# Block 1's values made 512 columns wide in six PSUM banks, the first key tile ahead of them, the gating in the last step and behind

## The chip, the cores and the metric

The kernel runs on one core of a Trainium2 chip. TensorE (PE) multiplies into PSUM, VectorE (DVE), ScalarE (ACT) and GpSimd (POOL) do the elementwise work, and SyncE's queue (SP) issues nearly all of the transfers. The metric is the device time of one execution in microseconds, as the median of several runs.

## What is computed

Two transformer blocks on 512 positions of 1024 channels, in fp32. The change is in the first block. `h` is the normalised, modulated input and `hc` the same for a context of 256 positions. From `h` come queries, keys, values and the inputs of a spatial gating and of a convolution; from `hc` come keys and values only. Cut to what matters:

```
h  = _modulate(_rmsnorm(x, norm1_g[l]), mod_l[0], mod_l[1])
hc = _modulate(_rmsnorm(xc, norm1_g[l]), mod_c[0], mod_c[1])
z  = h @ w_in[l]
q, k, v = _heads(z[..., :ATT_W]), _heads(z[..., ATT_W:2*ATT_W]), _heads(z[..., 2*ATT_W:3*ATT_W])
kvc = hc @ w_in[l][:, ATT_W:3 * ATT_W]
kc, vc = _heads(kvc[..., :ATT_W]), _heads(kvc[..., ATT_W:])
att = _neighbourhood_attention(q, k, v, kc, vc, na_rpb[l], rows)
y   = _mix_out(att, z, ...)      # joins att, the gating and the convolution
```

Here `ATT_W` is 512 (8 heads of 64). The gating mixes positions within chunks of 128 by a learned matrix and multiplies the result by `gelu(u)`; the convolution has 31 taps for each channel.

## The kernel before

**Precision and weights.** Every fp32 product is made of three matmuls (`mm3`): each operand is split into a high half (ScalarE, a copy to fp32r) and a low half (VectorE, the difference), and high by high, high by low and low by high are summed in a PSUM bank. The weights come through a stream `ws`: pieces of up to 1 MB are loaded by SP into `wraw`, and units of 128 by 1024 numbers are split into `whi` and `wlo`. `need(u)` asks for units two ahead of the one in use and loads one or two pieces beyond, in the order in which the `Proj` objects were made.

**Order.** The program is written out by hand; each engine works through its instructions in that order. PSUM has eight banks, given out by `bank()` from one pool; a bank is reused when the last reader of its former tile is done. Work that has no place of its own, above all the 62 convolution taps (`tap_v`, on VectorE, tile `cacc`), lies in a list `lv`, and `tick(part)` puts some of it into the order: at the rate of this stage, 3.3 x part / 0.75 taps.

**The stage in question.** Two tiles of queries for each of two weight pieces are projected. Between them `make_hc(*ks)` builds `hc[k]`: VectorE scales the context `cs`, ScalarE writes the high half, VectorE the low one; the last call makes `hc[5]` to `hc[7]` behind the last query tile. `ada_tick` puts eight modulation matmuls (`adab`) between. Then come the values. They are made in two halves of 256 columns, in tiles of 128 positions: four from `h` and two from `hc` for each half, each tile 8 steps of `mm3` in a bank of its own and split at once (`v_tile`). `split(*vn[i], vt_[i])` prepares the gating's operand, `gating(0)` and `gating(1)` each put 12 matmuls into two `mix` banks, add a bias on VectorE (tile `sgo`) and multiply by `u` on GpSimd. The generator `keys()` makes four tiles of keys, each step three matmuls with `h[k]` (512 columns, bank `k`) and three with `hc[k]` (256 columns, bank `kc`). Its first tile is taken ahead of the fourth tile of the second half, the others are spread over the attention, three or two steps a turn. Between the value tiles stand twelve copies of half tiles on GpSimd (`vs`), which shift values by 64 positions.

**The attention** runs over 32 turns (8 heads, 4 blocks). Turn n does the scores (`s`), the softmax (VectorE, ScalarE; GpSimd scales tile `e` by the reciprocal sum), and three turns later TensorE transposes it (`pt`). Everything on GpSimd goes in the order written.

Of the kernel before, what the change touches and what calls it, by code (L numbers as in the profile page):

```python
# [15 lines left out]
P = 128  # L16
T = 512
D = 1024
KD = D // P
# [112 lines left out]
def program(ctx: ExitStack, tc: tile.TileContext, A, outT):  # L132
# [14 lines left out]
    def bank(name="bank", cols=T):  # L147
        return ps.tile([P, cols], F32, tag="b", name=name, padded_shape=[P, T])

    def slot(dt=F32, name="slot", cols=T):  # L150
        t = sl.tile([P, T], dt, tag="s", name=name)
        return t if cols == T else t[:, :cols]

    def pair(name, cols=T):
        return slot(F32R, name + "_hi", cols), slot(F32R, name + "_lo", cols)


    def mm3(out, lhs, rhs, start, stop, **kw):

        PE.matmul(out, lhs[0], rhs[0], start=start, stop=False, **kw)  # L160
        PE.matmul(out, lhs[0], rhs[1], start=False, stop=False, **kw)  # L161
        PE.matmul(out, lhs[1], rhs[0], start=False, stop=stop, **kw)  # L162

    def split(hi, lo, src, scale=None, eng=None):

        if scale is None:
            S.activation(hi, src, AF.Copy)  # L167
            (eng or V).tensor_sub(lo, src, hi)  # L168
        else:
            S.activation(hi, src, AF.Copy, scale=scale)  # L170
            V.scalar_tensor_tensor(lo, src, scale, hi, op0=ALU.mult, op1=ALU.subtract)
# [49 lines left out]
    ws = Stream()  # L221
# [58 lines left out]
    def take(gen, n):  # L280

        for _ in range(n):
            if next(gen, None) is None:
                return

    class Later:
# [8 lines left out]
        def tick(self, part=1.0):  # L295
            self.due += self.rate * part
            while self.todo and self.due >= self.todo[0][0]:
                cost, fn, a = self.todo.pop(0)
                self.due -= cost
                fn(*a)  # L300
            if not self.todo:
                self.due = 0.0
# [44 lines left out]
    def doubled(parts):  # L347

        out = [(a, slot(F32R, "dbl")) for a in parts]
        for a, b in out:  # L350
            move(b[TOP], a[LOW])
            move(b[LOW], a[LOW])
        yield 1
        for a, b in out:
            move(a[LOW], a[TOP])
        yield out

    def stacked(hi, lo, other):

        move(other[TOP], hi[LOW])  # L360
        move(other[LOW], lo[LOW])
        yield 1
        move(hi[LOW], lo[TOP])
        yield hi, other
# [3 lines left out]
    def put_later(to, i, gen):  # L368

        left = [1]  # L370
        to[i] = None

        def step():
            if left:
                left.pop()
                return
            r = next(gen)
            if r != 1:
                to[i] = r
                later.remove(step)  # L380

        later.append(step)
# [22 lines left out]
    w_in, w2 = A["w_in"], A["w_in_2"]  # L405
    p_u = Proj(w_in, 1536, 8)
    p_q = [Proj(w_in, 256 * i, 8) for i in range(2)]
    p_v = [Proj(w_in, 1024 + 256 * i, 8, wide=True) for i in range(2)]
    p_k = [Proj(w_in, 512 + 256 * i, 8) for i in range(2)]
    p_out = [Proj(A["w_out"], 256 * i, 8) for i in range(4)]  # L410
    p_up = [[Proj(A["ffn_w_up"], c + 256 * j, 8) for c in (0, FF)] for j in range(KF // 2)]
    p_down = [Proj(A["ffn_w_down"], 256 * i, KF) for i in range(4)]
# [40 lines left out]
    def pc(name, i, n=1):  # L453
        a = PCOL[name][0]
        return par[:, a + i : a + i + n]
# [49 lines left out]
    h = [None] * KD  # L505
# [84 lines left out]
    def ada_end():  # L590
        r, t = ada_ends.pop(0)
        b = ada_bank.pop(r)
        for q in range(4):
            PE.matmul(b[:, 4 * q : 4 * q + 4], t[:, q * P : (q + 1) * P], pick, start=True, stop=True)
        for g in (0, 2):
            j = 4 * ROUNDS[r][g]
            V.tensor_add(mod[:, j : j + 8].rearrange("p (g q) -> p g q", q=4),
                         b[:, :16].rearrange("p (q g) -> p g q", g=4)[:, g : g + 2],
                         pc("ada_b", j, 8).rearrange("p (g q) -> p g q", q=4))
# [3 lines left out]
    def ada_tick(n=2):  # L603

        if ada_ends:
            ada_end()
        for _ in range(min(n, len(ada_live))):
            ada_step()
            ada_fetch()
# [138 lines left out]
    vt_ = []  # L748
    for i in range(4):
        b = bank("vgT", cols=256)  # L750
# [9 lines left out]
    hc = [None] * KD  # L760
# [19 lines left out]
    vn = []  # L780
# [15 lines left out]
    def gating(pr):  # L796
        for n2 in range(2):
            b = bank("mix")
            for n in range(2):
                lhs = [vn[2 * n2 + n][q][:, pr * P : (pr + 1) * P] for q in range(2)]  # L800
                mm3(b[:, n * 256 : (n + 1) * 256], lhs, [q[:, pr * 256 : (pr + 1) * 256] for q in sgp], True, True)
            for gg in range(2):
                r = slice(64 * gg, 64 * gg + 64)
                bv = b.rearrange("p (n g q) -> p g n q", n=2, g=2)[r, gg]
                ov = sgo[pr].rearrange("p (n q) -> p n q", q=P)[r, 2 * n2 : 2 * n2 + 2]
                bb = rows[1][r, pr * P : (pr + 1) * P].unsqueeze(1).to_broadcast([64, 2, P])
                V.tensor_add(ov, bv, bb)
        G.tensor_mul(sgo[pr], sgo[pr], u[pr])
# [17 lines left out]
    vt = [pair(f"v{i}") for i in range(4)]  # L826
    vc = [pair(f"vc{i}") for i in range(2)]
    vs = [pair(f"vs{i}") for i in range(3)]

    def keys():  # L830
        for i in range(4):
            b, bc_ = bank("k"), bank("kc", cols=CTX)
            for k in range(KD):
                w_ = p_k[i // 2].part(i % 2, k)
                mm3(b, w_, h[k], k == 0, k == KD - 1)
                mm3(bc_, w_, hc[k], k == 0, k == KD - 1)
                yield 6
            nat, other = pair("k"), slot(F32R, "k")
            split(*nat, b)
            t = slot(F32R, "kc")  # L840
            kcp[i] = t[:, :CTX], t[:, CTX:]
            for o, r in zip(kcp[i], (TOP, LOW)):
                split(o[TOP], o[LOW], bc_[r])

            put_later(kp, i, stacked(*nat, other))
            if i == 0:
                put_later(qp, i, doubled(qp[i]))
            tick(1.5 if i else 0)
        h.clear()
        hc.clear()  # L850

    def v_tile(pj, half, src, i, dst):
        cols = slice(256 * half, 256 * half + 256)
        b = bank("v", cols=256)
        for k in range(KD):
            mm3(b, [src[k][q][:, i * P : (i + 1) * P] for q in range(2)], pj.part(0, k, 256), k == 0, k == KD - 1)
        split(dst[0][:, cols], dst[1][:, cols], b)
        tick(0.5)

    for i in range(4):  # L860
        v_tile(p_v[0], 0, h, i, vt[i])
        split(*vn[i], vt_[i])
        if i % 2:
            ada_tick()
    for i in range(2):
        v_tile(p_v[0], 0, hc, i, vc[i])
    kg = keys()

    ws.limit = p_k[0].at[0, 0][0] + 1
    for i in range(4):  # L870
        if i == 3:
            take(kg, KD + 1)
        v_tile(p_v[1], 1, h, i, vt[i])
        if i in (0, 2):
            gating(i // 2)
        if i == 1:
            ada_end()
    for i in range(3):
        for q in range(2):
            G.tensor_scalar(vs[i][q][0:64, :], vt[i][q][64:128, :], 1.0, 0.0, op0=ALU.mult, op1=ALU.add)  # L880
            G.tensor_scalar(vs[i][q][64:128, :], vt[i + 1][q][0:64, :], 1.0, 0.0, op0=ALU.mult, op1=ALU.add)
    for i in range(2):
        v_tile(p_v[1], 1, hc, i, vc[i])
    ws.limit = 1 << 30
    del vn, sgp, vg, vt_, xs
    cs.clear()

# [150 lines left out]
    for n in range(NA + OUT + 2):  # L1038
        if n < NA:
            hp, blk, j = place(n)  # L1040
            if n in QD:
                i = 1 + QD.index(n)
# [37 lines left out]
        for i, steps in PLAN.get(n, ()):  # L1080
            if len(begun) == i:
                b = bank()
# [336 lines left out]
    for n in range(32 + O2 + 2):  # L1419
# [17 lines left out]
        q = n - O2  # L1437
# [201 lines left out]
```

## Time and profile before

| | |
|---|---|
| median of 3 runs | 1387.32 us (1387.29 to 1387.36) |
| profiled execution | 1388.53 us, its span 1386.1 us |
| TensorE busy | 1371.3 us (99% of the span) |
| VectorE, ScalarE, GpSimd busy | 778.7, 560.1, 228.4 us |
| mean granted TensorE clock | 0.997 |

The span runs from the first to the last instruction that the profiler saw; the execution's own time is 2.4 us more. A busy share counts an engine as busy from the start of an instruction to its end, and matmuls overlap, so two matmuls that start 0.23 us apart may each be 0.39 us long. How fast TensorE goes is seen by the distance from start to start. The stage of the change lies between 100 and 180 us of the span.

### The profile page before, as it was taken

How to read it: one execution, taken by the hardware profiler on the slowest of the kernel's cores; microseconds unless marked ns; L12 is line 12 of the kernel's file. 1: busy time of each engine (PE TensorE's matmuls, PEld its weight loads, DVE VectorE, ACT ScalarE, POOL GpSimd, SP SyncE). 2: the span in 40 equal slices, each digit the busy share in tenths (PEclk: the TensorE clock that was granted, in tenths of full speed). 3: DMA queues.
4: the chain of work that ended last, by engine and by line, in shares of the span. 5: the costliest groups of instructions: out<-in, count | busy, mean ns of one | idle time of the engine just before them, and what ended most of it. 6: DMA issues, size and time to landing. Idle time of an engine off the chain costs nothing.

```text
span 1386.1 us, 18747 instructions
## 1 busy us (share of the span) xinstructions
PE 1371.3 (99%) x7468; PEld 1151.3 (83%) x7468; DVE 778.7 (56%) x1158; ACT 560.1 (40%) x901; POOL 228.4 (16%) x252
## 2 busy tenths in 40 slices
PE   9999999999999999999999999999999999999997
PEld 5768999898888888888888888888897888888887
DVE  4479788465444443434458863635378866663223
ACT  4433258445333333323355543323454544343231
POOL 0032324101111110111133312000231111110100
PEclk9999999999999999999999999999999999999998
DMA  9992452323232222322273122333212332222221
GB/s 347 367 370 95 116 140 67 122 92 98 85 122 92 91 93 83 106 85 91 84 199 109 51 92 76 107 111 102 92 62 68 123 113 93 91 84 84 84 84 61
DMA packets 140886, 160.41 MB, mean 116 GB/s; under 512 B 5632, under 2 KB 117504, under 8 KB 140800
## 3 DMA queue, kind: packets, MB, share of 16 engines
q1 hardware_dynamic: 139360, 156.91, 35.1%
q10 hardware_dynamic: 1440, 2.31, 0.5%
q8 instruction: 58, 0.95, 0.3%
q14 instruction: 28, 0.23, 0.1%
HBM read 147.67 MB, written 2.10 MB: 108 GB/s over the span
## 4 chain that ended last, share of the span: by engine, by line
PE 88%; issue 4%; DVE 4%; POOL 2%; ACT 1%; DMA 1%; POOLq 0%; ACTq 0%
PE bank L160 23%; PE bank L162 23%; PE bank L161 23%; PE first L565 3%; PE v L160 1%; PE v L162 1%; PE v L161 1%; PE adab L484 1%; PE s L907 1%; PE pt L935 1%; DMA ada<-in_ada_first 1%; DVE wlo L209 1%; PE f L160 1%; PE f L161 1%; PE f L162 1%
## 5 line engine op out<-in xcount | busy, mean ns | idle before, releaser
L209 DVE TENSOR_TENSOR wlo<-wraw,whi 128x1024 fp32r<-128x1024 f32 (+1 forms) x211 | 276.0, 1316 | 117.2 <-ACT whi L201 117.0
L162 PE MATMUL bank<-h_hi,wlo 128*128 128x512 f32 (+1 forms) x816 | 304.2, 373 | 1.7 <-DVE wlo L209 1.7
L161 PE MATMUL bank<-h_lo,whi 128*128 128x512 f32 (+1 forms) x816 | 305.6, 374 | 0.2
L160 PE MATMUL bank<-h_hi,whi 128*128 128x512 f32 (+1 forms) x816 | 305.0, 374 | 0.0
L201 ACT ACTIVATE whi<-wraw 128x1024 fp32r<-128x1024 f32 (+1 forms) x211 | 217.1, 1035 | 99.3 <-PE bank L161 85.2
L160 PEld LDWEIGHTS bank<-h_hi,whi 128*128 128x128 f32 x816 | 153.6, 188 | 30.1 <-PE adab L484 1.7
L162 PEld LDWEIGHTS bank<-h_hi,wlo 128*128 128x128 f32 x816 | 153.6, 188 | 29.5 <-DVE wlo L209 2.5
L161 PEld LDWEIGHTS bank<-h_lo,whi 128*128 128x128 f32 x816 | 153.5, 188 | 28.1 <-DVE h_lo L1505 0.3
L168 POOL TENSOR_TENSOR act_lo<-cv,act_hi 128x512 fp32r<-128x512 f32 x44 | 61.3, 1393 | 428.9 <-ACT act_hi L167 428.9
L160 PE MATMUL bank<-act_hi,whi 128*128 128x512 f32 x308 | 119.8, 389 | 0.0
L161 PE MATMUL bank<-act_lo,whi 128*128 128x512 f32 x308 | 119.8, 389 | 0.0
L162 PE MATMUL bank<-act_hi,wlo 128*128 128x512 f32 x308 | 119.8, 389 | 0.0
L160 PE MATMUL bank<-hb_hi,whi 128*128 128x512 f32 x288 | 115.9, 403 | 0.3 <-DVE wt_lo L1400 0.3
L162 PE MATMUL bank<-hb_hi,wlo 128*128 128x512 f32 x288 | 112.6, 391 | 0.0
L161 PE MATMUL bank<-hb_lo,whi 128*128 128x512 f32 x288 | 112.5, 391 | 0.0
L167 ACT ACTIVATE act_hi<-cv 128x512 fp32r<-128x512 f32 x44 | 27.8, 633 | 129.4 <-DVE cv L1230 73.0
L161 PEld LDWEIGHTS bank<-act_lo,whi 128*128 128x128 f32 x308 | 57.8, 188 | 12.1
L162 PEld LDWEIGHTS bank<-act_hi,wlo 128*128 128x128 f32 x308 | 57.8, 188 | 12.0
L160 PEld LDWEIGHTS bank<-act_hi,whi 128*128 128x128 f32 x308 | 57.8, 188 | 11.9
L162 PEld LDWEIGHTS bank<-hb_hi,wlo 128*128 128x128 f32 x288 | 54.1, 188 | 11.6
L160 PEld LDWEIGHTS bank<-hb_hi,whi 128*128 128x128 f32 x288 | 54.1, 188 | 10.1 <-DVE wt_lo L1400 0.4
L161 PEld LDWEIGHTS bank<-hb_lo,whi 128*128 128x128 f32 x288 | 54.2, 188 | 9.1
(388 smaller groups left out, 2412.9 us busy)
## 6 DMA issues: line engine op xcount, KB each, us to landing
wraw<-in_w_in SPq DMA_DIRECT2D x23, 1024.0 KB, 5.5
wraw<-in_ffn_w_up SPq DMA_DIRECT2D x22, 1024.0 KB, 5.1
wraw<-in_w_up SPq DMA_DIRECT2D x22, 1024.0 KB, 5.1
ada<-in_ada_w SPq DMA_DIRECT2D x64, 256.0 KB, 5.7
ada<-in_ada_first SPq DMA_DIRECT2D x32, 256.0 KB, 6.0
wraw<-in_w_out SPq DMA_DIRECT2D x8, 1024.0 KB, 5.0
wraw<-in_ffn_w_down SPq DMA_DIRECT2D x8, 1024.0 KB, 5.0
wraw<-in_w_down SPq DMA_DIRECT2D x8, 1024.0 KB, 5.3
```

What stands on the lines that cost most here:

```text
L160: PE.matmul(out, lhs[0], rhs[0], start=start, stop=False, **kw)
L161: PE.matmul(out, lhs[0], rhs[1], start=False, stop=False, **kw)
L162: PE.matmul(out, lhs[1], rhs[0], start=False, stop=stop, **kw)
L167: S.activation(hi, src, AF.Copy)
L168: (eng or V).tensor_sub(lo, src, hi)
L201: S.activation(h, src, AF.Copy)
L209: V.tensor_sub(l, src, h)
L484: PE.matmul(out[32 * g : 32 * g + 32, : rhs.shape[1]], sc[:, kk, :], rhs, start=start, stop=stop, tile_position=(0, 32 * g), skip_group_ch ...
L565: PE.matmul(first[m], w_[:, m * P : (m + 1) * P], h[k][a], start=s0 and k == 0, stop=s1 and k == KD - 1)
L907: PE.matmul(st_s[n][:, ks], qp[hp][a][j][:, qs], k_, start=a == 0, stop=a == 1)
L935: PE.transpose(pt[:, c * P : (c + 1) * P], e[:, c * P : (c + 1) * P], ident)
```

## The change

The values become one projection of 512 columns: for each of the 8 steps, six `mm3` into six banks, four from `h` and two from `hc`. All six tiles are split behind the last step. The key weights are cut into pieces of 128, 128 and 256 columns, with the first ahead of the values, and the whole first key tile (its splits too) stands ahead of the values; a `yield 0` keeps the second tile's first step out of it. The splits of `vn` go into the first four value steps, `ada_tick` behind the steps 1 and 3, `ada_end` behind 5, `gating(0)` behind step 6, and `gating(1)` behind the splits of the values. `tick(0.75)` eight times takes the place of `tick(0.5)` twelve times. The limit on the weight stream in this stage falls away.

```diff
-    p_v = [Proj(w_in, 1024 + 256 * i, 8, wide=True) for i in range(2)]
-    p_k = [Proj(w_in, 512 + 256 * i, 8) for i in range(2)]
+
+    p_k = [Proj(w_in, 512, 8, P)]
+    p_v = Proj(w_in, 1024, 8, 512, wide=True)
+    p_k += [Proj(w_in, 512 + P, 8, P), Proj(w_in, 768, 8)]
+    k_tile = (p_k[0], 0), (p_k[1], 0), (p_k[2], 0), (p_k[2], 1)
...
-                w_ = p_k[i // 2].part(i % 2, k)
+                w_ = k_tile[i][0].part(k_tile[i][1], k)
...
             tick(1.5 if i else 0)
+            if i == 0:
+                yield 0
...
-    for i in range(4):
-        v_tile(p_v[0], 0, h, i, vt[i])
-        split(*vn[i], vt_[i])
-        if i % 2:
+    kg = keys()
+    take(kg, KD + 1)
+    vb = [bank("v") for _ in range(6)]
+    for k in range(KD):
+        w_ = p_v.part(0, k, 512)
+        for i, b in enumerate(vb):
+            mm3(b, [q[:, i % 4 * P : (i % 4 + 1) * P] for q in (h if i < 4 else hc)[k]], w_, k == 0, k == KD - 1)
+        if k < 4:
+            split(*vn[k], vt_[k])
+        if k in (1, 3):
             ada_tick()
-    for i in range(2):
-        v_tile(p_v[0], 0, hc, i, vc[i])
-    kg = keys()
-
-    ws.limit = p_k[0].at[0, 0][0] + 1
-    for i in range(4):
-        if i == 3:
-            take(kg, KD + 1)
-        v_tile(p_v[1], 1, h, i, vt[i])
-        if i in (0, 2):
-            gating(i // 2)
-        if i == 1:
+        if k == 5:
             ada_end()
+        if k == 6:
+            gating(0)
+        tick(0.75)
+    for i, b in enumerate(vb):
+        split(*(vt[i] if i < 4 else vc[i - 4]), b)
+    del vb, b
+    gating(1)
...
-    for i in range(2):
-        v_tile(p_v[1], 1, hc, i, vc[i])
-    ws.limit = 1 << 30
```

Three places show what moves. The first is TensorE behind the last query tile (tile `bank`). Before, the modulation is followed by values from `h` (the last row stands for the rest of the tile):

```order
L162 MATMUL bank<-h_hi,wlo 128x512
L484 MATMUL adab<-ada,sc 32x512 x8
L160 MATMUL v<-whi,h_hi 128x256
L161 MATMUL v<-wlo,h_hi 128x256
L162 MATMUL v<-whi,h_lo 128x256
```

In the change the key tile stands there:

```order
L162 MATMUL bank<-h_hi,wlo 128x512
L487 MATMUL adab<-ada,sc 32x512 x8
L160 MATMUL k<-h_hi,whi 128x512
L161 MATMUL k<-h_lo,whi 128x512
L162 MATMUL k<-h_hi,wlo 128x512
L160 MATMUL kc<-hc,whi 128x256
L161 MATMUL kc<-hc,whi 128x256
L162 MATMUL kc<-hc,wlo 128x256
```

The first reader of `hc` has moved to right behind the queries.

The second is VectorE at the same point, as one piece with the rows of the change: the splits of the last query tile, five taps, and the last call of `make_hc` (three scalings `cs`, three low halves `hc`), then what stands behind them.

```order
L171 SCALAR_TENSOR_TENSOR q_lo<-bank,q_hi 128x512
L209 TENSOR_TENSOR wlo<-wraw,whi 128x1024
L705 SCALAR_TENSOR_TENSOR cacc<-ag,par,cacc 128x506
L705 SCALAR_TENSOR_TENSOR cacc<-ag,par,cacc 128x505
L705 SCALAR_TENSOR_TENSOR cacc<-ag,par,cacc 128x504
L705 SCALAR_TENSOR_TENSOR cacc<-ag,par,cacc 128x503
L705 SCALAR_TENSOR_TENSOR cacc<-ag,par,cacc 128x502
L767 SCALAR_TENSOR_TENSOR cs<-cs,gs,rcbs 128x256 x3
L773 SCALAR_TENSOR_TENSOR hc<-cs,mod_115,hc 128x256 x3
L168 TENSOR_TENSOR k_lo<-k,k_hi 128x512
L168 TENSOR_TENSOR kc<-kc 64x256 x2
```

Up to the three `hc` the rows are those of before; behind them stood a weight unit and the first value's low half, and now stand the key tile's low halves.

The third is VectorE between the first gating and the attention's first softmax (tile `e`) in the change.

```order
L810 TENSOR_TENSOR sgo<-mix,rows 64x256 x4
L705 SCALAR_TENSOR_TENSOR cacc<-ag,par,cacc 128x511 x2
L705 SCALAR_TENSOR_TENSOR cacc<-ag,par,cacc 128x510
L705 SCALAR_TENSOR_TENSOR cacc<-ag,par,cacc 128x509
L705 SCALAR_TENSOR_TENSOR cacc<-ag,par,cacc 128x508
L705 SCALAR_TENSOR_TENSOR cacc<-ag,par,cacc 128x507
L168 TENSOR_TENSOR v_lo<-v,v_hi 128x512 x4
L168 TENSOR_TENSOR vc_lo<-v,vc_hi 128x512 x2
L810 TENSOR_TENSOR sgo<-mix,rows 64x256 x4
L209 TENSOR_TENSOR wlo<-wraw,whi 128x1024
L911 ISA e,nm<-s,bias 128x512
```

Before, both groups of `sgo` stood ahead of the first key tile's low halves, and every value tile had its low half right behind its matmuls.

## Rows read from the trace of the kernel before

**Rows 1.** The page: busy time, share of the span and instructions of each engine.

```profile
PE 1371.3 (99%) x7468; PEld 1151.3 (83%) x7468; DVE 778.7 (56%) x1158; ACT 560.1 (40%) x901; POOL 228.4 (16%) x252
```

**Rows 2.** What TensorE waited for, 100 to 250: us in total, times, longest.

```profile
PE pt L935 <- POOL e L928: 0.9, 3, 0.4
```

**Rows 3.** Busy time by stretch: us, then each engine's with its instructions, clock, DMA.

```profile
100.00:143.00 43.00, 43.00 (x336) 35.73 (x337) 41.07 (x71) 14.05 (x29) 10.33 (x13) 1.00 0.32 110
143.00:162.00 19.00, 19.00 (x136) 17.82 (x135) 11.42 (x21) 2.01 (x5) 9.65 (x14) 1.00 0.33 77
```

**Rows 4.** Order of time, TensorE: start, length; first of 72 value matmuls, then the scores.

```profile
153.27 0.28 PE L160 MATMUL v<-whi,h_hi 128*128 128x256 f32 x1
...
161.91 0.28 PE L907 MATMUL s<-k_hi,q_hi 128*128 128x256 f32 x1
```

**Rows 5.** The same, the second block's values: the first and last of 48 matmuls.

```profile
655.57 0.39 PE L160 MATMUL v<-whi,hb_hi 128*128 128x512 f32 x1
...
666.22 0.39 PE L162 MATMUL v<-whi,hb_lo 128*128 128x512 f32 x1
```

**Rows 6.** The same, the keys: first matmul of the first tile, and of the second.

```profile
143.82 0.40 PE L160 MATMUL k<-h_hi,whi 128*128 128x512 f32 x1
...
152.22 0.40 PE L160 MATMUL k<-h_hi,whi 128*128 128x512 f32 x1
```

**Rows 7.** First value matmul in order of time; tile `v`: matmuls from `hc`, first and last start.

```profile
109.97 0.39 PE L160 MATMUL v<-whi,h_hi 128*128 128x256 f32 x1
...
L160 PE MATMUL v<-whi,hc x32: 280/283/386, 125.6 to 161.5; 128*128 128x256 f32 x32
```

**Rows 8.** Order of time: VectorE, and ScalarE's last three `hc` (in brackets idle before).

```profile
116.09 3.86 DVE L702 SCALAR_TENSOR_TENSOR cacc<-ag,par,cacc 128x506 f32<-128x506 f32 x5
119.86 1.27 DVE L764 SCALAR_TENSOR_TENSOR cs<-cs,gs,rcbs 128x256 f32<-128x256 f32 x3
121.05 1.27 DVE L770 SCALAR_TENSOR_TENSOR hc<-cs,mod,hc 128x256 fp32r<-128x256 f32 x3
...
120.38 1.31 ACT L768 ACTIVATE hc<-cs,mod 128x256 fp32r<-128x256 f32 x3 [6.06 <-DVE cs L764]
```

**Rows 9.** Order of time, TensorE: the first transposition of the attention.

```profile
173.27 0.60 PE L935 MATMUL pt<-ident,e 128*128 128x128 f32 x4
```

**Rows 10.** Order of time, VectorE: `vn`, taps, the gating's adds, a key tile's low half.

```profile
125.57 0.42 DVE L168 TENSOR_TENSOR vn<-vgt,vn 128x256 fp32r<-128x256 f32 x1
...
130.10 2.28 DVE L702 SCALAR_TENSOR_TENSOR cacc<-ag,par,cacc 128x497 f32<-128x497 f32 x3
...
140.19 1.74 DVE L807 TENSOR_TENSOR sgo<-mix,rows 64x256 f32<-64x256 f32 x4
...
152.70 0.69 DVE L168 TENSOR_TENSOR k_lo<-k,k_hi 128x512 fp32r<-128x512 f32 x1 [3.67 <-ACT k_hi L167]
```

**Rows 11.** Order of time, GpSimd: second gating, copies `vs`, first scaling of the softmax.

```profile
149.16 1.28 POOL L808 TENSOR_TENSOR sgo<-sgo,u 128x512 f32<-128x512 f32 x1 [5.82 <-issue]
...
152.58 0.61 POOL L881 TENSOR_SCALAR vs_lo<-v_lo 64x512 fp32r<-64x512 f32 x1
153.25 0.61 POOL L880 TENSOR_SCALAR vs_hi<-v_hi 64x512 fp32r<-64x512 f32 x1
...
158.52 0.94 POOL L881 TENSOR_SCALAR vs_lo<-v_lo 64x512 fp32r<-64x512 f32 x1
169.47 1.03 POOL L928 TENSOR_SCALAR e<-e,rd 128x512 f32<-128x512 f32 x1 [10.01 <-DVE rd L923]
```

**Rows 12.** The page: loads of one weight, KB each, us from issue to landing.

```profile
wraw<-in_w_in SPq DMA_DIRECT2D x23, 1024.0 KB, 5.5
```

**Rows 13.** A stretch at the end (columns as in rows 3); TensorE's first matmuls, two groups.

```profile
1375.00:1380.00 5.00, 1.96 (x14) 1.57 (x13) 2.52 (x8) 0.90 (x3) 0.97 (x1) 0.77 0.00 0
...
1.49 3.78 PE L490 MATMUL junk<-ident 128*128 128x128 f32 x16 [1.49 <-POOL ident L463]
...
14.34 1.16 PE L400 MATMUL bc<-ident,ro 128*128 128x128 f32 x8
```

More of the change, by code (lines that the diff above doesn't have):

```diff
@@ L848, in keys @@
             tick(1.5 if i else 0)
+            if i == 0:
+                yield 0
         h.clear()
         hc.clear()
[L852 to L858, printed above, removed]
-    for i in range(4):
-        v_tile(p_v[0], 0, h, i, vt[i])
-        split(*vn[i], vt_[i])
-        if i % 2:
-            ada_tick()
-    for i in range(2):
-        v_tile(p_v[0], 0, hc, i, vc[i])
-    kg = keys()
-    ws.limit = p_k[0].at[0, 0][0] + 1
-    for i in range(4):
-        if i == 3:
-            take(kg, KD + 1)
-        v_tile(p_v[1], 1, h, i, vt[i])
-        if i in (0, 2):
-            gating(i // 2)
-        if i == 1:
-            ada_end()
+    kg = keys()
[8 more added lines that the diff above has]
+        if k in (1, 3):
+            ada_tick()
+        if k == 5:
+            ada_end()
+        if k == 6:
[5 more added lines that the diff above has]
+    gating(1)
     for i in range(3):
```

## The prediction

> **What bounds the kernel now.** I read the page first. TensorE is busy for 99% of the span, VectorE for 56% [rows 1]. Then I asked what TensorE waits for in the stretch round the change: 0.9 us in 150, all of it on three GpSimd results in the attention [rows 2]. So whatever the change takes off TensorE's own work or adds to its waits there shows in the end, nearly in full, because TensorE is the bound before and behind as well. The third view, busy time by stretch, says where the danger is: from 100 to 143 us VectorE has hardly a hole (41.07 of 43), and only from 143 to 162 it has room (11.42 of 19) [rows 3]. What the change asks of VectorE early comes late; what it pushes behind 143 us leaves room unused that was there.
>
> **Wider values: a gain.** Before, the values are 12 tiles of 24 matmuls of 256 columns, 288; now 144 of 512. What counts is the distance from start to start. 72 matmuls of 256 columns follow each other from 153.27 to the first scores at 161.91, so 8.64/72 = 0.120 us each [rows 4]. The values of the second block are already made with 512 columns: 48 in a row from 655.57 to 666.22, 10.65/47 = 0.2266 us [rows 5]. Sum: 288 x 0.1200 - 144 x 0.2266 = 34.56 - 32.63 = 1.9 us gained. The other bound is the 512-column matmuls of a key tile: a step of three of 512 and three of 256 takes 1.05 us (eight steps from 143.82 to 152.22 [rows 6]), which leaves 0.23 for a wide one, and a gain of 1.4. I take 1.9; rows 5 are the same form. The Trainium skill (TensorE: Matmul & The Clock Gate, "Wait — 56ns, not 53.3ns?") gives a fixed 2.5 ns per matmul over one column per cycle; an estimate by that page is 0.109 and 0.216 us, and a gain of only 0.4. The trace's matmuls of this form cost more apiece than the page says, and the rows decide.
>
> **The keys' first tile ahead: a wait.** Its eight steps are the same work, 8.4 us, now where the values began, at 109.97 [rows 7], plus 0.1 for the first matmul. Step k needs the normalised context hc[k], and hc[5..7] are made by the call right ahead, at the back of VectorE's queue. In the order of the change nothing ahead of these on VectorE moves, and in the trace that queue has no hole: five taps of the long convolution, 3.86 us from 116.09 on, and only at 119.86 the scaling of cs[5..7]; ScalarE makes the high halves from 120.38 (three in 1.31, the first there at 120.8), VectorE the low ones from 121.05 (three in 1.27, the first at 121.5) [rows 8]. Before, this cost nothing, because the value tiles of x ran meanwhile and hc was first read at 125.6 [rows 7]. Now step 5 reaches its context matmuls at 110.07 + 5 x 1.05 + 0.70 = 116.0; the first can go at 120.8, the second, which reads the low half, at 121.5 where it would have gone at 116.1. Loss: 5.3 us. Bounds: 4.8 if the high half alone held it, 6.2 if all three low halves (122.3) had to be there. Behind the waiting matmul stand steps 6 and 7 (whose hc is there by then) and all the values. VectorE has worked off its queue meanwhile.
>
> **Six banks held to the end: a small wait.** The program has eight PSUM banks. Six values and the two of the second gating fill them, so the first scores need the first value's bank back. TensorE would be at these scores at 161.91 [rows 4] - 1.05 (one key step now stands behind them) - 1.9 + 5.3 = 164.3; the last value step began 12 x 0.120 + 18 x 0.2266 = 5.5 us earlier, at 158.8. On VectorE stand, from then on, the second half of the first gating's adds (0.87, half of four at 1.74), six taps at 0.76 (2.28 for three), and only then the first value's low half, 0.69 [rows 10]: 158.8 + 0.1 + 0.87 + 4.56 + 0.69 = 165.0. Wait: 0.7 us; between nothing (should fewer taps stand there) and 4 (should scores need the last bank).
>
> **The gating behind: a wait on GpSimd.** VectorE then does five more low halves (3.45) and the second gating's adds (1.74): 170.2. GpSimd works in order, and its order did not change: the second gating's multiply (1.28), twelve half copies vs, then the scaling of the first softmax [rows 11]. Before, it began that multiply at 149.16, with half a key tile and three value tiles still ahead of the scores, and sat idle 10.0 us before the first scaling. Now it starts at 170.2. A copy takes 0.61 and the next starts 0.67 behind it where VectorE is quiet; beside taps one takes 0.94, so 1.0 apart: 8.0 to 12.0 us for twelve; I take 9.4, a third slow, since taps, wlo and low key halves run then. With 1.03 for the scaling the first softmax is ready at 170.2 + 1.3 + 9.4 + 1.0 = 181.9. TensorE wants to transpose it 11.36 us behind the first scores (161.91 to 173.27 [rows 4, 9]), at 176.4. Wait: 5.5 us; bounds 4.1 and 8.1, by the copies alone. Behind it stand key steps, scores and everything else on TensorE.
>
> **Nothing.** The same eight weight units are split; the loads are five instead of four and stay two ahead, each hidden by a unit's 8 us of matmuls (one lands 5.5 us after its issue [rows 12]; a late one would cost up to that). The splits of vn (0.42 on VectorE [rows 10]) and the taps (3.3 a step, 2.5 us) lie beside value steps of 18 x 0.2266 = 4.1 us; without that cover each split would cost its 0.42. The key tile's moves for the SP queue are asked for earlier and nothing there waits on them. The key step that goes into the attention is in the sum above.
>
> **TensorE's clock.** At the end of the span, from 1375 to 1380, TensorE is busy for 1.96 us of 5 and the mean granted clock is 0.77: for nearly half of that stretch it was at the lower level (1.2 GHz) [rows 13]. At the start 16 matmuls of 128 columns took 3.78 us, where 8 later took 1.16, so 16 would take 2.3: 1.5 us lost until the engine is up to speed. A pause of about 5 us may do the same, and the change makes two. I count one such fall, 1.5 us; bounds 0 and 3. The Trainium skill (the same page, "What's actually happening") has the half clock as TensorE's idle state, released by activity; the trace's end agrees.
>
> **Sum.** -1.9 + 5.3 + 0.7 + 5.5 + 1.5 = +11.1 us. The profiled execution took 1388.5 us (span 1386.1), so the like would take 1399.6; the median of the runs is 1387.3, so I predict 1398.4, +0.8%.
>
> **Rivals.**
> - *Neither wait, not slower*: hc[5] is there by 116.1 and the first softmax by 176.4, and only the wider values count: 1387.3 - 1.9 = 1385.4. It decides if VectorE comes to cs[5] nearly 5 us sooner than in rows 8. For it: TensorE had no wait here before. Against it: even without the five taps it would be 1 us late, and nothing in the change takes them away. 0.07; by 0.14% it would pass as no change (within 0.2%, about what a measurement can tell), and faster only if later attention waits fell too.
> - *One of the two waits alone*: the copies overlap differently, or hc is early. 1387.3 - 1.9 + 5.3 + 0.7 = 1391.4, or with the GpSimd wait alone 1391.6; a fall of the clock makes it 1393. Against it: the two have different causes and both queues are in order. 0.17.
> - *Both waits, all at their worst*: copies slow throughout, two falls: 1387.3 - 1.4 + 6.2 + 0.7 + 8.1 + 3 = 1403.9. 0.06.
> - *The forecast*, both waits with none, one or two falls (1396.9 to 1399.9): 0.70. By the page's fixed cost per matmul it would be 1.5 later, which no row of this form supports.
>
> The range from 1391 to 1403 leaves out the first and most of the third. Slower by over 0.2% holds all but the first and a remainder of mistakes in my reckoning: 0.89; same 0.08; faster 0.03.
>
> **What would show it.** In the profile after: matmuls v of 512 columns 0.227 apart; a TensorE wait of about 5 us on hc (line of make_hc) near 116 us; first scores near 165; a wait of pt on GpSimd's e near 176 to 182, with the copies vs from about 171; a granted clock under 1.00 in one or both pauses. I am wrong if hc[5] comes before 117, if the copies vs begin well before 170, or if waits in the attention shrink by what these cost.

## The result, and the profile after

The changed kernel takes 1404.38 us (median of 4 runs, 1403.85 to 1405.32), the kernel before, run beside it, 1387.34 us (1387.29 to 1388.2): ratio 1.0122, 95% interval 1.0109 to 1.0136. It is 17.0 us slower, where the prediction had +11.1 with a range that ended at 1403.0. The profiled execution took 1404.74 us, its span 1403.0, mean granted clock 0.992.

The page's line of busy time answers to [rows 1]. TensorE has 144 matmuls fewer and yet is busy 2.3 us longer:

```profile
PE 1373.6 (98%) x7324; PEld 1146.9 (82%) x7324; DVE 781.0 (56%) x1152; ACT 559.7 (40%) x895; POOL 230.2 (16%) x252
```

What TensorE waited for from 100 to 260 us (total, times, longest), where [rows 2] had 0.9 in all:

```profile
PE pt L931 <- POOL e L924: 7.9, 5, 6.7
PE kc L160 <- ACT hc L771: 4.8, 1, 4.8
PE s L903 <- DVE v_lo L168: 1.9, 1, 1.9
```

All three forecast waits are there. The rows add up to 14.6 us; less the 0.9 of before and the 1.5 that the wider values give back, they explain 12.2 of the 17. The windows show where to look for the rest (columns as in [rows 3]):

```profile
100.00:118.80 18.80, 15.44 (x89) 10.17 (x81) 17.57 (x28) 5.00 (x9) 9.39 (x12) 1.00 0.54 191
118.80:125.60 6.80, 5.35 (x16) 4.48 (x17) 2.88 (x8) 1.94 (x5) 0.00 (x0) 0.50 0.16 54
125.60:165.00 39.40, 39.40 (x198) 30.07 (x197) 26.44 (x40) 9.36 (x17) 1.79 (x1) 1.00 0.34 98
165.00:183.60 18.60, 13.12 (x82) 11.46 (x80) 16.51 (x31) 7.53 (x14) 9.86 (x12) 1.00 0.33 92
183.60:190.50 6.90, 3.73 (x13) 3.25 (x14) 4.29 (x7) 1.41 (x3) 4.71 (x5) 0.51 0.29 79
```

In two stretches the granted clock (last column but two) is 0.50: TensorE runs at 1.2 GHz. Each begins while it waits and reaches beyond the wait. In order of time, TensorE (start, length; in brackets the idle time before):

```profile
115.05 0.39 PE L162 MATMUL k<-h_hi,wlo 128*128 128x512 f32 x1
120.19 0.58 PE L160 MATMUL kc<-hc,whi 128*128 128x256 f32 x1 [4.75 <-ACT hc L771]
120.83 0.58 PE L161 MATMUL kc<-hc,whi 128*128 128x256 f32 x1
121.42 0.63 PE L160 MATMUL k<-h_hi,whi 128*128 128x512 f32 x1
121.85 0.63 PE L161 MATMUL k<-h_lo,whi 128*128 128x512 f32 x1
...
123.34 0.63 PE L160 MATMUL k<-h_hi,whi 128*128 128x512 f32 x1
...
125.90 0.39 PE L162 MATMUL v<-whi,h_lo 128*128 128x512 f32 x1
...
168.30 0.39 PE L903 MATMUL s<-k_hi,q_hi 128*128 128x256 f32 x1 [1.93 <-DVE v_lo L168]
...
186.77 1.11 PE L931 MATMUL pt<-ident,e 128*128 128x128 f32 x4 [6.73 <-POOL e L924]
...
192.12 0.40 PE L903 MATMUL s<-k,dbl 128*128 128x256 f32 x2
```

Behind the first pause two 512-column matmuls start 0.43 us apart (121.42, 121.85), not 0.227 as in [rows 5]. A whole key step takes 1.92 us there (121.42 to 123.34) and 1.05 at the full rate [rows 6], so 0.45 of the time at the half rate is lost. Work resumed at 120.19 and waited once more, some 0.5 us, for the low half of `hc` (the second `kc` matmul starts at 120.83, 0.64 behind the first). From there to 125.6, where the clock rose, are 4.8 us: 2.2 lost. Behind the second pause, from 186.77 to 190.5, are 3.7 us: 1.7 lost. Together 3.9 us, an estimate from these rows; an experiment below, in which the clock stays up, gives the same.

VectorE and GpSimd in order of time, from the first gating to the first softmax:

```profile
161.93 0.75 DVE L705 SCALAR_TENSOR_TENSOR cacc<-ag,par,cacc 128x511 f32<-128x511 f32 x1
162.05 1.79 POOL L811 TENSOR_TENSOR sgo<-sgo,u 128x512 f32<-128x512 f32 x1 [50.14 <-DVE sgo L810]
162.72 1.67 DVE L705 SCALAR_TENSOR_TENSOR cacc<-ag,par,cacc 128x511 f32<-128x511 f32 x1
164.42 1.54 DVE L705 SCALAR_TENSOR_TENSOR cacc<-ag,par,cacc 128x510 f32<-128x510 f32 x2
...
171.15 1.73 DVE L810 TENSOR_TENSOR sgo<-mix,rows 64x256 f32<-64x256 f32 x4
172.91 1.22 DVE L209 TENSOR_TENSOR wlo<-wraw,whi 128x1024 fp32r<-128x1024 f32 x1
173.01 2.28 POOL L811 TENSOR_TENSOR sgo<-sgo,u 128x512 f32<-128x512 f32 x1 [9.17 <-DVE sgo L810]
175.38 0.93 POOL L879 TENSOR_SCALAR vs_hi<-v_hi 64x512 fp32r<-64x512 f32 x1
...
184.14 1.49 POOL L880 TENSOR_SCALAR vs_lo<-v_lo 64x512 fp32r<-64x512 f32 x1
185.73 2.75 POOL L924 TENSOR_SCALAR e<-e,rd 128x512 f32<-128x512 f32 x3
```

Read it as a relay. The multiply asks at 162.05, while a tap runs until 162.68; it ends at 163.84, 1.16 behind the tap (alone it took 1.28 [rows 11]). The next tap starts at 162.72 and takes 1.67 instead of 0.75: it too got its turn only when the multiply was nearly done. At 173.01 the second multiply asks beside the split of a weight unit that runs until 174.13, and ends 1.16 behind that. Of two such instructions one stands still while the other works. The Trainium skill (SBUF — State Buffer, "SBUF: two separate sides") describes that: VectorE and GpSimd share a pair of ports, and of an instruction of VectorE with two inputs in SBUF and one of GpSimd that reads SBUF, the one that starts first holds it for its whole length. These rows agree, apart from the 0.1 to 0.2 us by which two of them overlap.

### The profile page after: what moved, and what is told of

Read it like the earlier page. It is cut to its first block, busy times and chain, and to the rows that moved or that the text cites. A ratio compares the mean times of both kernels' runs of the same rounds, so it can differ in the third digit from the quotient of the medians.

```text
span 1403.0 us, 18451 instructions
## 1 busy us (share of the span) xinstructions
PE 1373.6 (98%) x7324; PEld 1146.9 (82%) x7324; DVE 781.0 (56%) x1152; ACT 559.7 (40%) x895; POOL 230.2 (16%) x252
## 4 chain that ended last, share of the span: by engine, by line
PE 83%; DVE 6%; issue 4%; DMA 2%; POOL 2%; ACT 2%; POOLq 0%; SPq 0%; ACTq 0%; DVEq 0%
PE bank L160 22%; PE bank L162 22%; PE bank L161 22%; PE first L568 3%; PE v L160 1%; DVE wlo L209 1%; PE v L161 1%; PE v L162 1%; DVE cacc L705 1%; DMA ada<-in_ada_w 1%; DMA ada<-in_ada_first 1%; PE pt L931 1%; PE f L160 1%; PE f L161 1%; PE f L162 1%
## 5 line engine op out<-in xcount | busy, mean ns | idle before, releaser
L162 PE MATMUL bank<-h_hi,wlo 128*128 128x512 f32 (+1 forms) x816 | 304.2, 373 | 1.7 <-DVE wlo L209 1.7
L162 PEld LDWEIGHTS bank<-h_hi,wlo 128*128 128x128 f32 x816 | 153.6, 188 | 29.4 <-DVE wlo L209 2.5
L162 PE MATMUL bank<-act_hi,wlo 128*128 128x512 f32 x308 | 119.8, 389 | 0.0
L162 PE MATMUL bank<-hb_hi,wlo 128*128 128x512 f32 x288 | 112.6, 391 | 0.0
L162 PEld LDWEIGHTS bank<-act_hi,wlo 128*128 128x128 f32 x308 | 57.8, 188 | 12.1
L162 PEld LDWEIGHTS bank<-hb_hi,wlo 128*128 128x128 f32 x288 | 54.1, 188 | 11.6
```

## The experiments

Diffs are against the changed kernel, unless another is named. "Relative" times count from the first value or key matmul behind the queries, since the start-up of single executions differs (it stands at 109.97 before, 109.22 after, and between 109.16 and 110.02 in the others). So counted, the last transposition of the stage stands at 135.7 before and at 153.1 after, +17.3.

### One cause at a time

**The context's last part made one tile earlier.**

```diff
-        make_hc(*((5, 6, 7) if m else (3, 4)))
+        if not m:
+            make_hc(3, 4, 5, 6, 7)
```

> All of hc[3] to hc[7] is made one query tile sooner, ahead of the last query tile's five taps; nothing else changes. If the wait of TensorE on hc and the fall of the clock inside it are a cost of their own, the pause of 4.8 us near 115 us goes, 0.5 us for the low half goes, and with them the lower clock from 118.8 to 125.6 (about 2.5 us lost), while the two later waits (1.9 us for the first value's bank, 6.7 us for the first transposition) and the second fall stay: 1404.4 - 7.8 = 1396.6. If the clock's fall costs nothing: 1399.1. If VectorE's queue is late anyway and the wait only moves to a bank or a weight unit behind the key tile: over 1402.

Measured: 1399.06 us (1398.68 to 1399.39), ratio 1.0081 (1.0066 to 1.0096), 5.3 us less than the changed kernel. The wait on `hc` is gone, and the clock's first fall with it:

```profile
PE pt L932 <- POOL e L925: 8.3, 5, 6.7
PE s L904 <- DVE v_lo L168: 1.9, 1, 1.9
```

The first scores come 7.7 us earlier (relative 51.4 for 59.1): 4.75 and 0.5 for the wait and 2.2 for the clock, and 0.2 that were not followed. That is what was expected, but less of it reached the end: the second fall cost 2.1 here instead of 1.7 (half rate until 184.6, work resumed at 179.9; 0.45 of 4.7), later waits of `pt` took 1.6 instead of 1.2, and this execution's start-up was 0.8 longer.

**The taps of the last two value steps moved into the six ahead.**

```diff
-        tick(0.75)
+        tick(1.0 if k < 6 else 0)
```

> The same number of taps, but all in the first six value steps, none behind the first or second gating. VectorE then reaches the values' low halves 5.6 us sooner. If the taps are what holds the first bank and, through the second gating's adds, GpSimd: the scores' wait of 1.9 us goes, and GpSimd starts its last multiply at about 168 in place of 173, so the first transposition comes 4.7 us sooner: 1399.7, or 1397.8 if its pause is then too short for the clock to fall. If GpSimd's copies alone set that transposition, whenever they start: only the bank's wait shrinks and is lost again at the transposition, 1404.

Measured: 1400.77 us (1400.24 to 1402.27), ratio 1.0095 (1.008 to 1.011), and 1400.38 (1400.01 to 1401.11) in a second series:

> The kernel with the taps moved alone, once more, on the same chip as the one with the filled pauses: 1400.8 us as in the run before of it (1400.24 to 1402.27), with the half rate behind both pauses. It says whether the clock falls at the same places and how far single executions differ.

3.6 to 4.0 us came back, about 1 less than expected. The causes are as named: the scores' wait is gone and that of `pt` is 2.4 shorter. The profiled execution, the quickest of its series, has 4.5 back in its span.

The waits that are left (the first series):

```profile
PE pt L931 <- POOL e L924: 5.9, 5, 4.3
PE kc L160 <- ACT hc L771: 4.7, 1, 4.7
```

The taps stood ahead of the values' low halves, and those ahead of the second gating, so they delayed both. The two profiles of this kernel have the same waits and different clocks: behind the first pause the half rate lasted until 124.9 where work resumed at 120.8 in one, and in the other from 121.2 to 124.6, some 1.6 and 1.5 us lost.

**The second gating behind GpSimd's copies.** The line `gating(1)` moves from behind the splits of the values to behind the loop of the twelve `vs` copies.

> The twelve copies vs stand ahead of the second gating in GpSimd's order; VectorE and TensorE keep theirs. If the order on GpSimd is the cause of the last wait: the copies begin near 168 with the first low halves in place of 175.4, the multiply follows them, the first scaling comes by about 180 as TensorE wants it, and the wait of 6.7 us with its fall of the clock (1.9) goes: 1395.9. If the copies' own length or VectorE's lateness sets it: no more than 2 us, 1402 or over.

Measured: 1398.39 us (1398.27 to 1400.01), ratio 1.008 (1.0063 to 1.0097). The wait of `pt` falls from 7.9 to 1.4 in all, which is the cause named, but the gain is 6.0 us where 8.5 was expected. Most of what is missing went to a new place, in the windows and in the waits:

```profile
169.80:173.20 3.40, 3.40 (x13) 2.92 (x12) 3.34 (x8) 0.00 (x0) 3.09 (x6) 0.50 0.01 2
```

```profile
PE s L903 <- DVE v_lo L168: 2.4, 1, 2.4
```

The scores now wait 2.4 us instead of 1.9, and the clock falls behind this pause, which it did not in the changed kernel: 0.45 of 3.4 us, 1.5.

### The clock's share by itself

**Needless matmuls in the two long pauses** (their results go to a bank that nobody reads).

```diff
+    def fill(n):
+        fb_ = bank("fill")
+        for _ in range(n):
+            PE.matmul(fb_, h[0][0][:, :P], h[0][0], start=True, stop=True)
...
+                if i == 0 and k == 5:
+                    fill(20)
                 mm3(bc_, w_, hc[k], k == 0, k == KD - 1)
...
+        if n == LAG:
+            fill(28)
         if 0 <= n - LAG < NA:
             att_turn(n - LAG)
```

> Needless matmuls (20 and 28 of 512 columns, 4.5 and 6.3 us at 0.227 each) stand where TensorE pauses, ahead of the context matmuls of step 5 and ahead of the first transposition, into a bank that nobody reads. The waits on hc and GpSimd end when they did. If the falls of the clock cost about 2.5 and 1.9 us on top of the pauses: no fall, 1404.4 - 4.4 = 1400.0. If the lower clock costs nothing because other engines set the pace there: 1404. If the fillings make the waits longer: over 1405.

Measured: 1401.52 us (1400.72 to 1402.05), ratio 1.0098 (1.0083 to 1.0113): 2.9 us less than the changed kernel, though TensorE does more and nothing else was changed. But it is inconclusive as to size, since the clock fell behind the third pause instead, that of the scores, where 0.45 of 3.4 us, 1.5, is lost (a window):

```profile
166.50:170.00 3.50, 3.50 (x12) 3.11 (x13) 3.49 (x7) 0.00 (x0) 0.00 (x0) 0.51 0.00 0
```

So the same was tried where that pause is gone: the taps moved as above, `fill(20)` and, for the shorter wait, `fill(17)`.

> The changed kernel with the taps of the last two value steps moved ahead (that takes away the scores' wait, and leaves a wait of 4.7 us on hc and one of 4.3 us on the first softmax), and with needless matmuls in those two pauses: 20 of 128x512 ahead of the waiting context matmuls, 17 ahead of the first transposition; nothing else differs from the kernel with the taps moved alone, and the waits should end when they did. If the clock's falls behind the pauses are what the first sum missed (rows at the half rate: about 2.5 us behind the first pause, 1.7 behind the second), the clock stays at 1.00 in the whole stage and the time is 4.2 us under that of the kernel with the taps moved alone: 1396.6 us. If one fall of 1.5 us was all there was to have, 1399.3. If the matmuls only lengthen the waits, 1400.8 or more.

Measured: 1396.57 us (1396.32 to 1397.35, 5 runs), ratio 1.0066 (1.0053 to 1.0078); beside it, on the same chip, the taps moved alone 1400.38. The fill ends just as the awaited result comes, and the whole stage runs at full rate. First the window over the stage, then TensorE in order of time:

```profile
100.00:260.00 160.00, 158.25 (x1188) 135.30 (x1188) 126.08 (x266) 78.12 (x161) 48.30 (x60) 1.00 0.35 103
```

```profile
116.04 4.70 PE L836 MATMUL fill<-h_hi 128*128 128x512 f32 x20
120.95 0.38 PE L160 MATMUL kc<-hc,whi 128*128 128x256 f32 x1 [0.20 <-ACT hc L771]
...
124.50 0.39 PE L162 MATMUL v<-whi,h_lo 128*128 128x512 f32 x1
...
176.13 4.04 PE L836 MATMUL fill<-h_hi 128*128 128x512 f32 x17
180.55 0.66 PE L938 MATMUL pt<-ident,e 128*128 128x128 f32 x4 [0.38 <-POOL e L931]
...
184.19 0.40 PE L910 MATMUL s<-k,dbl 128*128 128x256 f32 x2
```

This checks the 3.9 us of the changed kernel. The first `v` matmul of L162 stands 3.55 us behind the first waiting `kc` matmul here (120.95 to 124.50) and 5.71 there (120.19 to 125.90): 2.2 lost. The scores shown last stand 3.64 us behind the first `pt` here and 5.35 there (186.77 to 192.12): 1.7.

The kernel with the taps moved alone (the second series) has 0.98 over the same stretch:

```profile
100.00:260.00 160.00, 149.14 (x1116) 127.71 (x1116) 123.03 (x263) 74.89 (x156) 48.31 (x60) 0.98 0.35 102
```

The fill saves 3.8 us by the medians: far nearer the 4.2 that were expected than the 1.5 of the prediction. Not all of it is the clock itself. In the two profiled executions the last transposition comes 3.7 sooner (relative 144.0 for 147.8): 3.0 by the two falls, compared matmul by matmul as above, and 0.7 because a later wait of `pt` is not there. The 4.2 had taken half of the stretches behind the pauses for lost, which is too much.

### VectorE against GpSimd

**GpSimd without the first gating's multiply** (that part of the computation is left out).

```diff
-        G.tensor_mul(sgo[pr], sgo[pr], u[pr])
+        if pr:
+            G.tensor_mul(sgo[pr], sgo[pr], u[pr])
```

> The changed kernel without GpSimd's multiply of the first gating by u (that part of the computation is left out). If GpSimd's work beside it is what makes the six taps take 0.93 us each in place of 0.76: they go back to 0.76, the first value's bank comes 1.0 us sooner (a wait of 0.9 in place of 1.9), and with it all behind: 1403.3. If the taps are slow for another reason: the same times as the changed kernel's.

Measured: 1404.29 us (1403.0 to 1404.99), ratio 1.0119 (1.0106 to 1.0133), no difference that the time could show, since single executions spread over 2 us. The trace does show it. Six taps take 4.67 us, where they took 5.59 (161.93 to 167.52) beside the multiply, and the scores wait 1.0 instead of 1.9. VectorE and GpSimd in order of time, and the wait:

```profile
161.87 4.67 DVE L705 SCALAR_TENSOR_TENSOR cacc<-ag,par,cacc 128x511 f32<-128x511 f32 x6
...
172.04 2.27 POOL L812 TENSOR_TENSOR sgo<-sgo,u 128x512 f32<-128x512 f32 x1 [59.69 <-PE s L904]
```

```profile
PE s L904 <- DVE v_lo L168: 1.0, 1, 1.0
```

The second multiply, still beside a weight unit's split, keeps its 2.27.

### All three mends, and the width by itself

**The three edits together** (context earlier, taps earlier, second gating behind the copies).

> The change with hc[3] to hc[7] one query tile sooner, the taps in the first six value steps and the copies vs ahead of the second gating. If the change is slow by its three waits and the clock that falls in them, and by nothing else, no pause is left and the wider values are all that stays: 1387.3 - 1.5 (the starts of the value matmuls as the changed kernel's trace has them) = 1385.8, under the kernel before. If something else in the new order costs, such as the key step that went into the attention or the six splits at once: over 1388.

Measured: 1386.91 us (1386.52 to 1387.91, 11 runs) beside 1387.72, ratio 0.9996 (0.9987 to 1.0005). 17.5 us of the changed kernel are gone, and what stays is no difference from before that can be told. Up to the first scores it is 2.6 us ahead of before (relative 49.3 for 51.9), of which 1.05 is the key step that was moved behind them; but at the last transposition only 0.7 (135.0 for 135.7). The key step is done in the attention, and the waits there rise from 0.9 [rows 2] to 1.8: 2.6 less 1.05 less 0.9 is the 0.7. The waits from 100 to 260, and the one that is new, in order of time on SyncE's queue, VectorE, GpSimd and TensorE:

```profile
PE pt L932 <- POOL e L925: 1.8, 4, 1.0
```

```profile
202.56 0.46 SPq L345 DMA_DIRECT2D k_hi<-k_lo  x1
203.07 0.58 SPq L822 DMA_DIRECT2D bias<-in_rpb  x1
...
206.78 0.69 DVE L912 CUSTOM_DVE_ANT_0 e<-s,bias 128x512 f32<-128x512 f32 x1 [2.19 <-DMA bias<-in_rpb]
...
209.53 1.29 POOL L168 TENSOR_TENSOR cat_lo<-sgo,cat_hi 128x512 fp32r<-128x512 f32 x1 [0.92 <-POOL e L925]
210.80 1.36 POOL L925 TENSOR_SCALAR e<-e,rd 128x512 f32<-128x512 f32 x2
211.55 0.66 PE L932 MATMUL pt<-ident,e 128*128 128x128 f32 x4 [0.97 <-POOL e L925]
```

The low half of the gating that GpSimd makes ahead of this scaling of `e` is not new: the kernel before has it at the same place. New is that VectorE's softmax waits 2.19 us for its `bias`, a tile that SyncE's queue loads. That load goes out behind the moves of a key tile, at 203.07. In the kernel before it goes out at the same time, but VectorE comes to that softmax 2.4 us later than it could here, and finds it loaded:

```profile
203.18 0.58 SPq L818 DMA_DIRECT2D bias<-in_rpb  x1
206.97 0.68 DVE L915 CUSTOM_DVE_ANT_0 e<-s,bias 128x512 f32<-128x512 f32 x1
```

So the load did not come sooner with the work. The wait of `pt` follows it: 2.19 us for the load and 0.97 for `pt` here, 1.94 and 0.73 with the taps moved alone (the second series), 1.53 and 0.29 in the changed kernel, 0.62 and none with the pauses filled. So much the traces show; no run moved the load.

**The same with each value `mm3` made as two of 256 columns** (two accumulations share a bank, and its sums differ; amount and order of the work are the same).

```diff
-            mm3(b, [q[:, i % 4 * P : (i % 4 + 1) * P] for q in (h if i < 4 else hc)[k]], w_, k == 0, k == KD - 1)
+            for cs_ in HALF:
+                mm3(b[:, cs_], [q[:, i % 4 * P : (i % 4 + 1) * P] for q in (h if i < 4 else hc)[k]], [w[:, cs_] for w in w_], k == 0, k == KD - 1, skip_group_check=True)
```

> The three mends, but each value matmul of 512 columns is two of 256 again (288 in all), in the same order and into the same banks. If the gain of the wider matmuls is what the distances say (0.120 for 256, 0.227 to 0.231 for 512): 1.3 to 1.9 us over the kernel with the three mends, 1387.1 to 1387.7. By the page's fixed 2.5 ns per matmul: 0.4 over it.

Measured: 1388.06 us (1387.63 to 1389.27), ratio 1.0004 (0.9995 to 1.0012). The scores come 1.6 us later (relative 50.9 for 49.3): that is the width's worth. The waits of `pt` fall from 1.8 to 1.1 (1.41 us for the load of `bias`, and 0.19 for `pt` behind it), and the medians show 1.15: a part of the gain is waited away. The Trainium skill's fixed 2.5 ns per matmul (TensorE: Matmul & The Clock Gate, "Wait — 56ns, not 53.3ns?") would by an estimate be 0.4; the measurement decides.

**Both gatings in the last two steps, no `gating(1)` behind**, with the context and the taps early, which leaves the order of the copies alone.

```diff
-        if k == 6:
-            gating(0)
+        if k > 5:
+            gating(k - 6)
```

> hc sooner, taps in the first six steps, and the second gating right behind the last value step, ahead of the values' splits, with both GpSimd multiplies ahead of the copies. If it is the place of the second gating that holds GpSimd: the copies begin with the values' low halves near 162 and the first scaling is in time, but the splits stand behind the second gating's adds, so the scores may wait 1 to 2 us for the first bank: 1386 to 1388. If the order of the copies is what counts: a wait of several us at the first transposition, 1390 or over.

Measured: 1389.29 us (1388.69 to 1389.78), ratio 1.0011 (1.0002 to 1.002), 2.4 us above the three mends, and above the lower figures expected. By the last transposition it is 1.5 behind (136.5 for 135.0), of which 0.8 is the first `pt` waiting for its softmax and 0.5 are two waits round the second gating. The copies' order counts for part of it still; the rest was not followed.

**The gating's low half on VectorE**, with the three mends and, as a control, in the kernel before.

```diff
-            split(*cat[4 + i], sgo[i], eng=G)
+            split(*cat[4 + i], sgo[i])
```

> The three mends, and besides the low halves of the gating's output (cat4 and cat5, 1.3 us each on GpSimd, in the middle of the attention) go to VectorE. In the trace of the three mends TensorE waits 1.1 us for a scaled softmax that stands behind one of them. If the gain of the wider values is given back there: that wait goes, and the time falls by about 1 us to 1385.9. If VectorE is then late for the next softmax: no change from 1386.9, or up.

> The kernel before with the same two low halves on VectorE, as a control: its own waits at that place are 0.5 and 0.2 us, so it should gain less, 0 to 0.6 us: 1387.1 to 1387.7. If it gains as much as the kernel with the mends, the wider values are worth nothing in the end.

Measured: 1387.68 us (1387.06 to 1388.53), ratio 0.9999 (0.9991 to 1.0008), and 1388.99 us (1388.38 to 1389.53), ratio 1.0009 (1.0 to 1.0018). A miss: the waits of `pt` are 2.0 and 2.1, where they were 1.8 and 0.9, and both kernels lose about 1 us by it. The two differ by 1.3, near the width's worth again. No version was found that is faster than before beyond what can be measured.

## Why the prediction was wrong

The sign, the three waits, their places and their causes were right; the time fell 1.4 us outside the range, because two kinds of terms were sized too small: the clock by 2.4 us, and the two terms in which VectorE and GpSimd work beside one another by 1.2 each. The measured column comes from the rows of after and the experiments.

| term | predicted | measured |
|---|---|---|
| wider values | -1.9 | -1.5 in the stage, -1.6 by the experiment |
| wait on `hc` | 5.3 | 4.75 and 0.5 |
| scores on the first value's bank | 0.7 | 1.9 |
| `pt` on GpSimd | 5.5 | 6.7 |
| TensorE's clock | 1.5 | 3.9 |
| not separated, 0.3 of it in later waits of `pt` | 0 | 1.0 |
| sum | 11.1 | 17.3 |

- **The step that failed is the clock's**: "I count one such fall, 1.5 us; bounds 0 and 3." There were two, one behind each long pause, and they cost 2.2 and 1.7, together more than the upper bound. The price had been read from the start of the span, where 16 short matmuls came 1.5 us late [rows 13]; but the profile gives no lower clock there (1.00 from 1.5 to 5.3 us), and the row says nothing of how long the half rate lasts behind a pause in the middle of the work. Here it went on for 5.4 and 3.7 us after work had resumed. Filling the pauses without shortening them gave 3.8 us back, and the profiles place 3.0 in the matmuls behind the pauses, so this is shown and not only argued. Had the falls cost no more than the 1.5 that was counted, and all else as it came, the time would have been 1402.0, inside the range.
- **The scores' wait** came out 1.2 larger. The step took "six taps at 0.76" from a row in which GpSimd did nothing [rows 10]. Beside the first gating's multiply six take 5.59, not 4.56. The experiment without the multiply brings 0.9 of it back.
- **The wait of `pt`** came out 1.2 larger, inside its bounds. The multiply was counted at 1.28 [rows 11] and took 2.28, because VectorE had begun a weight unit's split 0.1 us before it. The copies took 10.35 with their gaps (175.38 to 185.73), not 9.4: five of them ran at 0.93 or more, beside taps and a weight unit's split.
- **The wait on `hc`** was right to 0.1 us, with its mechanism: moving `make_hc` one tile ahead removes it whole.
- **The wider values** were 0.3 to 0.4 below the term and inside its bounds (1.4 to 1.9).
- **SyncE's queue** was put at nothing ("nothing there waits on them"). In the changed kernel that is nearly right: a softmax of the attention waits 1.53 us for its `bias` behind a key tile's moves, and TensorE 0.3 for it. In the kernel with the three mends the wait behind it is 1.0, more than half of what the wider values gain.
- **The landmarks** were late by the same terms: scores at 168.3 for 165, copies from 175.4 for 171, the wait of `pt` from 180.0 to 186.8 for 176.4 to 181.9. The rival nearest to the outcome was "both waits, all at their worst" with two falls, 1403.9, which was given 0.06; the two waits did not need their worst, since the two falls cost more than the 3 us they were given there.

## What to carry to other kernels

A wait on the bounding engine is not paid for with its own length alone: where TensorE stands still for some microseconds, price in the half rate behind it, 1.5 to 2.2 us a pause here, and count one for each pause. When work is moved to where VectorE and GpSimd both have elementwise work in SBUF, take neither's duration from a row in which the other was idle; add the lengths of those that meet. And a change that gathers work into one place (six banks held to the end, splits in a row, gating behind) should be read for what stood in the gaps it closes: here 1.6 us of real gain needed three moves of other code to be seen at all. Last, a gain in one stage is kept only if what the next stage waits for comes sooner too: here a load of `bias` did not.

## What the runs showed of the hardware

- The clock falls behind pauses of 4.3 to 6.7 us in every profile that has them unfilled, but in two experiments also behind the scores' pause, of 2.4 us (the copies first) and of 1.9 us (both long pauses filled); in the changed kernel itself the same pause of 1.9 us brought none. The Trainium skill (TensorE: Matmul & The Clock Gate, "What's actually happening") has the half rate as the idle state that activity ends; the rows agree: each fall begins in a pause or right behind one. What decides whether a short pause brings a fall stays open.
- What the fall behind one and the same pause of 4.7 us costs is not always the same: 2.2 us in the changed kernel, 1.6 and 1.5 in the two profiles with the taps moved. Part of the spread of single executions may come from there: of the eight executions with the taps moved, the three with a mean granted clock of 0.994 or 0.995 took 1400.01 to 1400.24 us, the five with 0.992 took 1400.4 to 1402.27. Both profiles are of the former, so their rows may show less than the medians hold.
- At the half rate, 0.45 of the time is lost: a key step takes 1.92 us for 1.05.
- VectorE and GpSimd took turns almost instruction by instruction: a multiply of 1.28 took 2.28 behind a split of 1.22, a tap of 0.75 took 1.67 behind a multiply.
